# A seven-product matmul chunk with its products in another order

## The chip, the cores and the metric

The kernel runs on one core of one Trainium2 chip. TensorE (PE) multiplies, VectorE (DVE), ScalarE (ACT) and GpSimd (POOL) work on tiles beside it, and SyncE (SP) issues the transfers. The metric is the device time of one execution in microseconds: the median of three runs. Beside it stands one profiled execution with its trace.

## The reference

What is computed is one decoder layer in float32, and a last norm, over 1024 tokens of width 1024:

```python
def sqrelu_mlp(h, w1, w2):
    return jnp.square(jax.nn.relu(h @ w1)) @ w2

x = x + gla_mixer(rms_norm(x, norm_mix), w_in, w_gk_up, b_gk, g_onorm, w_out)
x = x + sqrelu_mlp(rms_norm(x, norm_ffn), w_ff1, w_ff2)
return rms_norm(x, final_norm)
```

The mixer is gated linear attention with four heads. It ends with a product of its gated output (1024 x 1024) and `w_out` (1024 x 1024). The MLP multiplies the normed rows by `w_ff1` (1024 x 4096), takes the square of the positive part, and multiplies by `w_ff2` (4096 x 1024). `rms_norm` divides each row by the root of its mean square and multiplies it by a gain.

## The kernel before, in words

The first third of the run is the attention with its projections. The change does not touch it. Everything after it is nine large products of 1024 x 1024 by 1024 x 1024, called **chunks** here: chunk 0 is the projection through `w_out`, whose result is added to the rows of x and kept as `x1`; then come four pairs, of which one chunk goes up (a quarter of `w_ff1`, result: a quarter of the hidden layer, `hd`) and one goes down (the fitting quarter of `w_ff2`, result: added to `x1`). The list `plan` (L852 to L855) holds for each chunk its left and right side and its sink, the function that takes each finished block of results away.

**One chunk is seven products and not eight.** Each matrix is cut into 2 x 2 blocks of 512 x 512, named "11", "12", "21", "22", and the chunk is computed by the Strassen-Winograd scheme. A product has as operands a block or a sum of blocks, and the results are kept in seven running sums. `form` (L600) says what each product needs: numbers 0, 4 or 3, 5 take blocks as they are, others take the sum "t" or the blocks after "t" has been worked into them. Only the products 0 and 5 take blocks as they were loaded or computed on both sides; each of the others needs a sum on one side at least.

**A product** is 48 matmuls of 128x512: four column blocks ("lanes") of 128 by two halves of the inner dimension by two by three. There are three because each float32 operand is split in two parts of lower width, `hi` (a copy on ACT, L86) and `lo` (the rest, a subtraction on DVE, L87), and hi x hi, hi x lo and lo x hi are summed. A lane's sum lies in one bank of PSUM. `BANK = "UVUVUWU"` says to which of three families of banks each of the seven products adds: U has four banks of the kind "gl"; V and W have three of the kind "mm" and one "gl" each. There are five "gl" and three "mm" banks. Products of one family add to the same banks one after another, and after products 0 to 6 a sink reads the sums as they stand.

**What sets the order of the work.** On PE it is the order in which the code is written (`tc.manual_schedule` for PE). The other engines' queues are set by a scheduler that follows the order of the code and lets blocks marked `high_priority` go ahead. The loop at L889 runs over the chunks and, in each, over the products. Before a product is issued, `operand` issues the next one's sums (L623: weights' sums on POOL, activations' sums on DVE) and splits (L86, L87). So the operands of a product are made while the product before it runs. A weight's sums for the product after that one are issued there too. SP issues all transfers in order; the weights of the next chunk are loaded while the products 5 and 6 of a chunk run.

**Buffers.** A weight block lies in a tile "w8" (three buffers) or "v8" (two); the sum "t" of the weights takes a "w8" buffer. Sums of activations lie in "raw" tiles, split operands in "big" tiles (eight), the hidden layer and the normed rows of the first up chunk in "og" tiles.

**The norm between.** After chunk 0 the rows of `x1` are normed (`normed`, L756: add, square on ACT, root, scale on DVE) and turned around by transposes on PE (`transposed`, L764: four transposes of 128x128 fill one "mm" bank, and ACT copies it out at L773). Rows 0 to 3 are complete when product 5 has been added, rows 4 to 7 with product 6. The up chunk needs the turned rows as its right operand.

**The end.** In the last chunk the sink is `final` (L822): it adds to `x1`, takes the squares of one half of a row when that half is complete, and finishes the row (root, scale, two transfers out) with the other half.

Of the kernel before, what the change touches and what calls it, by code (L numbers as in the profile page):

```python
# [14 lines left out]
ALU = mybir.AluOpType  # L15
# [33 lines left out]
def hybrid_trunk(ctx: ExitStack, tc: tile.TileContext, x, xT, w_head, w_r, w_gk, w_up,  # L49
# [85 lines left out]
    def run(general):  # L135
# [461 lines left out]
        BANK = "UVUVUWU"  # L597
        ADD, SUB = ALU.add, ALU.subtract
# [135 lines left out]
        wo.load("12")  # L734
# [87 lines left out]
        def final(n, lane, p_):  # L822
# [5 lines left out]
            if n in (3, 4):  # L828
                y = new(ROW[t])
                y, sq = row[t] = flat(y) if ROW[t] == "t2" else y, new("st")  # L830
                act.activation(y[:, 512:], xt[:, 512:], AF.Square, accum_out=sq[:, 0:1])
                pool.tensor_scalar(sq[:, 3:4], sq[:, 0:1], 1.0 / D, EPS, op0=ALU.mult, op1=ALU.add)
                pool.tensor_scalar(sq[:, 4:5], sq[:, 3:4], -0.5, None, op0=ALU.mult)
                pool.tensor_tensor(xt[:, 512:], xt[:, 512:], gfin[0][:, 512:], op=ALU.mult)
            elif n in (5, 6):
                y, sq = row[t]
                with tc.high_priority():
                    act.activation(y[:, :512], xt[:, :512], AF.Square, accum_out=sq[:, 1:2])
# [5 lines left out]
                    act.activation(y[:, 512:], xt[:, 512:], AF.Copy, scale=rs)  # L844
                    nc.sync.dma_start(out[t * P:(t + 1) * P, 512:], y[:, 512:])
                    dve.scalar_tensor_tensor(y[:, :512], xt[:, :512], rs, gfin[0][:, :512], op0=ALU.mult, op1=ALU.mult)
                    nc.sync.dma_start(out[t * P:(t + 1) * P, :512], y[:, :512])
# [35 lines left out]
        def transposes_after(hf):  # L883
            def between(lane):
                if lane in (1, 2):
                    transposed(hf, range(4 * lane - 4, 4 * lane))
            return between
# [101 lines left out]
```

## Time and profile before

| | |
|---|---|
| median of 3 runs | 1057.83 us (1057.79 to 1059.22) |
| profiled execution | 1058.82 us, span 1057.1 us |
| PE busy | 1034.1 us, 98%, 5122 matmuls and transposes |
| weight load (PEld) | 876.4 us, 83% |
| DVE, ACT, POOL busy | 717.8 us (68%), 535.0 us (51%), 245.1 us (23%) |
| transfers | 127.65 MB, mean 121 GB/s |

The span is what the profile covers; the profiled execution took 1.7 us more than that. Busy times are sums over the run, so they say which engine has work nearly always and not where an engine waits. For that the stretches of the run are read one by one. The attention ends at about 334 us; chunk 0 and its norms lie between 334 and 441 us; the up and down chunks fill the rest. In a row of the groups or of the timeline stand the start, the length, the engine, the line, the operation, the tiles `out<-in`, their shape and the count, and in brackets the idle time ahead of it with what ended it. A tile's name is cut to its kind there: `gl` and `mm` are banks of PSUM, `big` split operands, `w` and `v` weights, `raw`, `og`, `qk` activations.

### The profile page before, as it was taken

The numbers are of one execution on the slowest core, as the hardware profiler recorded it, in microseconds if no ns is written. First come the engines' busy times: TensorE is split into PE (matmuls) and PEld (weight loads), VectorE is DVE, ScalarE is ACT, GpSimd is POOL, SyncE is SP. The second block draws the span as 40 slices with busy tenths as digits, with TensorE's granted clock in tenths as the row PEclk, the third lists the DMA queues.
The fourth block names the chain that finished last, engine by engine and source line by source line (L and its number), as shares of the span: only waits on it lengthen the run. The fifth ranks groups of instructions, "written<-read, shape, count | busy, mean of one in ns | idle before, by whom it ended". The sixth has DMA issues, their size and how long they took to land.

```text
span 1057.1 us, 13350 instructions
## 1 busy us (share of the span) xinstructions
PE 1034.1 (98%) x5122; PEld 876.4 (83%) x5122; DVE 717.8 (68%) x960; ACT 535.0 (51%) x922; POOL 245.1 (23%) x151
## 2 busy tenths in 40 slices
PE   9999999999999898989999999999999999999996
PEld 8989899899888787778888888888888888888885
DVE  7564747566658986788997336986329976249975
ACT  2645747576656244856733245533346432447355
POOL 0000101000002604324223403404312406222351
PEclk9999999999999998999999999999999999999999
DMA  8510111112115140287222656123664043753004
GB/s 290 201 41 21 44 38 40 41 41 80 61 40 200 40 120 15 96 337 262 67 65 62 272 200 238 40 80 120 226 259 171 20 120 112 285 201 119 1 1 162
DMA packets 61977, 127.65 MB, mean 121 GB/s; under 512 B 3920, under 2 KB 36816, under 8 KB 54736
## 3 DMA queue, kind: packets, MB, share of 16 engines
q1 hardware_dynamic: 61760, 126.70, 33.9%
q8 instruction: 42, 0.69, 0.3%
q14 instruction: 31, 0.25, 0.1%
q10 hardware_dynamic: 144, 0.01, 0.0%
HBM read 107.82 MB, written 18.87 MB: 120 GB/s over the span
## 4 chain that ended last, share of the span: by engine, by line
PE 89%; DVE 6%; ACT 2%; issue 2%; DMA 1%; SPq 0%; ACTq 0%; DVEq 0%
PE gl L77 46%; PE mm L77 41%; DVE big L87 2%; DVE raw L623 2%; DMA w<-in_w_out 1%; PE gl L461 1%; DVE og L623 0%; ACT qk L759 0%; DMA raw<-in_w_head 0%; DVE t L726 0%; DVE qk L726 0%; PE gl L363 0%; PE mm L771 0%; DVE qk L761 0%; ACT og L773 0%
## 5 line engine op out<-in xcount | busy, mean ns | idle before, releaser
L77 PE MATMUL gl<-big,big 128*128 128x512 f32 x2052 | 480.6, 392 | 5.8 <-DVE big L87 5.8
L77 PEld LDWEIGHTS gl<-big,big 128*128 128x128 f32 x2052 | 388.1, 189 | 87.6 <-DVE big L87 6.6
L77 PE MATMUL mm<-big,big 128*128 128x512 f32 x972 | 229.7, 389 | 0.6 <-DVE big L87 0.5
L77 PEld LDWEIGHTS mm<-big,big 128*128 128x128 f32 x972 | 182.3, 188 | 39.1 <-DVE big L87 1.4
L87 DVE TENSOR_TENSOR big<-w,big 128x1024 fp32r<-128x1024 f32 x90 | 130.7, 1482 | 96.6 <-ACT big L86 96.6
L77 PE MATMUL mm<-big,w 128*128 128x512 f32 x744 | 180.5, 393 | 0.8 <-ACT w L86 0.8
L86 ACT ACTIVATE big<-w 128x1024 fp32r<-128x1024 f32 x90 | 91.1, 1052 | 142.0 <-PE gl L77 141.5
L77 PEld LDWEIGHTS mm<-big,w 128*128 128x128 f32 x744 | 136.4, 188 | 27.3 <-ACT w L86 1.0
L623 POOL TENSOR_TENSOR w<-w,w 128x1024 f32<-128x1024 f32 x36 | 107.6, 2998 | 136.6 <-DVE big L87 126.5
L623 POOL TENSOR_TENSOR w<-w,v 128x1024 f32<-128x1024 f32 x18 | 45.8, 2557 | 313.4 <-DVE big L87 140.1
L87 DVE TENSOR_TENSOR big<-v,big 128x1024 fp32r<-128x1024 f32 x36 | 52.0, 1469 | 50.4 <-ACT big L86 50.4
L87 DVE TENSOR_TENSOR big<-og,big 128x1024 fp32r<-128x1024 f32 (+1 forms) x52 | 57.5, 1115 | 32.3 <-ACT big L86 32.1
L77 PE MATMUL mm<-w,big 128*128 128x256 f32 x576 | 73.0, 284 | 0.0
L86 ACT ACTIVATE big<-og 128x1024 fp32r<-128x1024 f32 (+1 forms) x52 | 47.4, 953 | 49.6 <-PE gl L77 49.4
L77 PEld LDWEIGHTS mm<-w,big 128*128 128x128 f32 x576 | 70.9, 192 | 0.2
L86 ACT ACTIVATE big<-raw 128x1024 fp32r<-128x1024 f32 (+1 forms) x42 | 38.6, 933 | 60.6 <-DVE raw L623 40.5
L623 POOL TENSOR_TENSOR w<-v,w 128x1024 f32<-128x1024 f32 x18 | 57.0, 3185 | 43.2 <-DVE big L87 43.2
L87 DVE TENSOR_TENSOR big<-raw,big 128x1024 fp32r<-128x1024 f32 (+1 forms) x42 | 61.4, 1481 | 0.0
L86 ACT ACTIVATE big<-v 128x1024 fp32r<-128x1024 f32 x36 | 36.2, 1049 | 38.0 <-PE gl L77 38.0
L86 ACT ACTIVATE w<-raw 128x1024 fp32r<-128x1024 f32 (+2 forms) x26 | 25.7, 993 | 39.6 <-PE mm L77 27.5
L794 ACT ACTIVATE og<-og 128x1024 f32<-128x1024 f32 x24 | 25.4, 1058 | 39.6 <-DVE og L787 39.6
L87 DVE TENSOR_TENSOR w<-raw,w 128x1024 fp32r<-128x1024 f32 (+2 forms) x26 | 29.6, 1141 | 14.1 <-ACT w L86 13.8
(206 smaller groups left out, 1017.6 us busy)
## 6 DMA issues: line engine op xcount, KB each, us to landing
big<-xv SPq DMA_DIRECT2D x42, 1024.0 KB, 6.8
xv<-big SPq DMA_DIRECT2D x14, 1024.0 KB, 5.1
v<-in_w_ff SPq DMA_DIRECT2D x32, 256.0 KB, 4.4
w<-in_w_ff SPq DMA_DIRECT2D x32, 256.0 KB, 3.8
w<-in_w_ff SPq DMA_DIRECT2D x16, 512.0 KB, 5.5
v<-in_w_ff SPq DMA_DIRECT2D x16, 512.0 KB, 4.4
raw<-in_w_head SPq DMA_DIRECT2D x15, 512.0 KB, 4.0
og<-in_x SPq DMA_DIRECT2D x8, 512.0 KB, 7.6
```

The costliest lines, as they stand in the source:

```text
L77: pe.matmul(o, w, m, start=start, stop=stop, skip_group_check=partial)
L86: act.activation(hi, src, AF.Copy)
L87: dve.tensor_tensor(lo, src, f32(hi), op=ALU.subtract)
L461: pe.transpose(tp[:, j * P:(j + 1) * P], on[:, j * P:(j + 1) * P], ident)
L623: self.eng.tensor_tensor(*(self.ap(b, kp, self.span) for b in (o, x_, y_)), op=op)
L794: act.activation(d2, d2, AF.Relu)
```

## The change

The seven products of each chunk are issued in the order 0, 5, 1, 2, 3, 4, 6 and no longer by their numbers. Below, "place" means the position in that order and a product's number its number in `form`. Products 0 and 5, which take plain blocks, now stand first and second. With that:

- a lane's bank is taken when its first matmul is issued, and no longer all four at the start of a product;
- the loads of the next chunk's weights go out as "11" and "12" at the sixth place and "21" and "22" at the seventh; in chunk 0 "21" is loaded second, where "12" was, and "12" and "22" follow after the rows of x;
- weights' sums for place k + 1 are issued together with the operands of place k, in every chunk (the first up chunk had an order of its own);
- rows 0 to 3 of `x1` are complete after product 3 (the fifth place) and their norm moves there; the norm of rows 4 to 7 stays with product 6;
- the transposes of rows 0 to 3 move from two groups of sixteen, inside the seventh product of chunk 0, to four groups of eight: two in the sixth and two in the seventh. Those of rows 4 to 7 move from two groups of sixteen in the first product of the up chunk to four groups of eight, two in its first and two in its second product;
- in `final` the halves of a row change roles where the other half is complete first.

```diff
         BANK = "UVUVUWU"
+        ORDER = (0, 5, 1, 2, 3, 4, 6)
...
-            if n in (0, 1, 5):
-                for lane in range(4):
-                    bank[b, lane] = new("gl" if b == "U" or lane == 3 else "mm")
+            def take(lane):
+                bank[b, lane] = new("gl" if b == "U" or lane == 3 else "mm")
 
             def products(lane, kh):
+                if n in (0, 1, 5) and kh == 0:
+                    take(lane)
...
         wo.load("11")
-        wo.load("12")
+        wo.load("21")
         ops = [(so.split(0), wo.split(0))]
         for t in (0, 4, 1, 5, 2, 6, 3, 7):
             load_x1(t)
-        wo.sums(1)
         for f in r3[4:]:
             f()
+        wo.load("12")
         wo.load("22")
-        wo.load("21")
...
-        def operand(i, n):
+        def operand(i, at):
 
             out = []
             for s in plan[i][:2]:
                 early = s is weight_of(i)
-                if n and not early:
-                    s.sums(n)
-                out.append(s.split(n))
-                if n < 6 and early:
-                    s.sums(n + 1)
+                if not early:
+                    s.sums(ORDER[at])
+                out.append(s.split(ORDER[at]))
+                if at < 6 and early:
+                    s.sums(ORDER[at + 1])
             return out
 
-        def norm_after(e):
+        def norm_after(last, e):
             def then(n, lane, p_):
                 onto_x1(n, lane, p_)
-                normed(4 * e + lane)
+                if n == last:
+                    normed(4 * e + lane)
             return then
...
+        between = {(0, 5, 2): (0, (0, 1)), (0, 5, 3): (0, (2, 3)), (0, 6, 0): (0, (4, 5)), (0, 6, 1): (0, (6, 7)),
+                   (1, 0, 2): (1, (0, 1)), (1, 0, 3): (1, (2, 3)), (1, 1, 0): (1, (4, 5)), (1, 1, 1): (1, (6, 7))}
 
         for i, (lhs, rhs, sink) in enumerate(plan):
-            for n in range(7):
+            for at, n in enumerate(ORDER):
                 cur = ops.pop(0)
-                if n == 5:
-                    load(i + 1, ("11", "12", "22") if i % 2 else ("11", "21", "22"))
-                if n == 6:
-                    load(i + 1, ("21",) if i % 2 else ("12",))
...
+                here = {lane: between[i, at, lane] for lane in range(4) if (i, at, lane) in between}
+                if at == 5:
+                    load(i + 1, ("11", "12"))
+                if at == 6:
+                    load(i + 1, ("21", "22"))
...
+                following = (i, at + 1) if at < 6 else (i + 1, 0)
+                if following[0] < len(plan):
+                    ops.append(operand(*following))
+                if i == 0 and at in (4, 6):
+                    sink = norm_after(n, at // 6)
+                elif i == 0:
+                    sink = onto_x1
+                step(n, *cur, sink, bool(here) or i == len(plan) - 1 and at == 6,
+                     lambda lane: lane in here and transposed(*here[lane]))
```

The first place where the order differs is POOL's queue at the start of chunk 0, its first weight sums (the numbers behind a tile's kind tell the buffers' uses apart). Before:

```order
L623 TENSOR_TENSOR w8566_3545<-w8553_3510,v8552_3507 128x1024 x2
L623 TENSOR_TENSOR w8566_3545<-w8571_3612,w8566_3545 128x1024
L623 TENSOR_TENSOR w8553_3510<-w8571_3612,w8553_3510 128x1024
L623 TENSOR_TENSOR w8566_3545<-w8571_3612,w8566_3545 128x1024
L623 TENSOR_TENSOR w8553_3510<-w8571_3612,w8553_3510 128x1024
L623 TENSOR_TENSOR w8566_3545<-v8572_3615,w8566_3545 128x1024 x2
```

And now:

```order
L624 TENSOR_TENSOR w8578_3651<-w8570_3609,v8552_3507 128x1024 x2
L624 TENSOR_TENSOR w8570_3609<-w8571_3612,w8570_3609 128x1024 x2
L624 TENSOR_TENSOR w8578_3651<-w8571_3612,w8578_3651 128x1024 x2
L624 TENSOR_TENSOR w8578_3651<-v8553_3510,w8578_3651 128x1024 x2
```

The sums are the same eight. The sum "t" is now `w8578`, made after the blocks `w8570` and `w8571` and not before them, so it has another buffer: the one of the weights of the last attention projection (`w8549`), where before it was that of the projection ahead of it (`w8545`).

The second place is PE around the end of chunk 0 and the transposes of rows 4 to 7 in the up chunk. Before, with the first and last of a group of sixteen:

```order
L77 MATMUL gl661_4314<-big656_4295,big629_4142 128x512 x6
L77 MATMUL gl661_4314<-big657_4298,big630_4145 128x512 x6
L771 MATMUL mm668_4347<-ident_71,c4632_4164 128x128
...
L771 MATMUL mm671_4365<-ident_71,qk653_4285 128x128
L77 MATMUL gl662_4315<-big656_4295,big629_4142 128x512 x6
L77 MATMUL gl662_4315<-big657_4298,big630_4145 128x512 x6
L771 MATMUL mm674_4386<-ident_71,c4632_4164 128x128
...
L771 MATMUL mm677_4404<-ident_71,qk653_4285 128x128
```

And now, from the third group on, in the second product of the up chunk, with the first and last of a group of eight:

```order
L77 MATMUL mm680_4423<-big660_4309,big657_4300 128x512 x6
L77 MATMUL mm680_4423<-big661_4312,big658_4303 128x512 x6
L772 MATMUL mm683_4439<-ident_71,c4639_4195 128x128
...
L772 MATMUL mm684_4445<-ident_71,qk654_4290 128x128
L77 MATMUL mm685_4451<-big660_4309,big657_4300 128x512 x6
L77 MATMUL mm685_4451<-big661_4312,big658_4303 128x512 x6
L772 MATMUL mm686_4467<-ident_71,c4639_4195 128x128
...
L772 MATMUL mm687_4473<-ident_71,qk654_4290 128x128
L77 MATMUL mm688_4479<-big660_4309,big657_4300 128x512 x6
```

The groups are half as long, and here the product around them has its own sums in "mm" banks (`mm680`, `mm685`, `mm688`), as the transposes have, where before it was a product with sums in "gl" banks.

The third place is ACT's queue there, the copies of those transposes (L774). Before, they stood in two groups of four (L773), and a split between:

```order
L773 ACTIVATE og667_4346<-mm670_4359,vec_63 128x512
L773 ACTIVATE og667_4346<-mm671_4365,vec_63 128x512
L86 ACTIVATE big680_4427<-raw678_4423 128x2x512
L785 ACTIVATE og665_4330<-gl662_4315 128x512
L773 ACTIVATE og672_4384<-mm674_4386,vec_63 128x512
```

And now:

```order
L774 ACTIVATE og668_4362<-mm673_4395,vec_63 128x512
L86 ACTIVATE big678_4415<-raw676_4411 128x2x512
L86 ACTIVATE big679_4418<-raw677_4412 128x2x512
L774 ACTIVATE og681_4437<-mm683_4439,vec_63 128x512
L774 ACTIVATE og681_4437<-mm684_4445,vec_63 128x512
```

Two splits of sums (`raw676`, `raw677`) now stand between the second and the third pair of copies.

More of the change, by code (lines that the diff above doesn't have):

```diff
@@ L827, in final @@
             onto_x1(n, lane, p_)
-            if n in (3, 4):
+            if n in (4, 5):
                 y = new(ROW[t])
                 y, sq = row[t] = flat(y) if ROW[t] == "t2" else y, new("st")
-                act.activation(y[:, 512:], xt[:, 512:], AF.Square, accum_out=sq[:, 0:1])
+                cs = half(dh)
+                act.activation(y[:, cs], xt[:, cs], AF.Square, accum_out=sq[:, 0:1])
                 pool.tensor_scalar(sq[:, 3:4], sq[:, 0:1], 1.0 / D, EPS, op0=ALU.mult, op1=ALU.add)
                 pool.tensor_scalar(sq[:, 4:5], sq[:, 3:4], -0.5, None, op0=ALU.mult)
-                pool.tensor_tensor(xt[:, 512:], xt[:, 512:], gfin[0][:, 512:], op=ALU.mult)
-            elif n in (5, 6):
+                pool.tensor_tensor(xt[:, cs], xt[:, cs], gfin[0][:, cs], op=ALU.mult)
+            elif n in (3, 6):
                 y, sq = row[t]
+                cs, was = half(dh), half(1 - dh)
                 with tc.high_priority():
-                    act.activation(y[:, :512], xt[:, :512], AF.Square, accum_out=sq[:, 1:2])
+                    act.activation(y[:, cs], xt[:, cs], AF.Square, accum_out=sq[:, 1:2])
                     act.activation(sq[:, 6:7], sq[:, 1:2], AF.Ln, scale=1.0 / D, bias=sq[:, 3:4])
@@ L843, in final @@
                     dve.scalar_tensor_tensor(rs, sq[:, 7:8], 1.5, sq[:, 6:7], op0=ALU.add, op1=ALU.mult)
[L844 to L847, printed above, removed]
+                    act.activation(y[:, was], xt[:, was], AF.Copy, scale=rs)
+                    nc.sync.dma_start(out[t * P:(t + 1) * P, was], y[:, was])
+                    dve.scalar_tensor_tensor(y[:, cs], xt[:, cs], rs, gfin[0][:, cs], op0=ALU.mult, op1=ALU.mult)
+                    nc.sync.dma_start(out[t * P:(t + 1) * P, cs], y[:, cs])
         hd = [{} for _ in range(NC)]
@@ L889, in run @@
         for i, (lhs, rhs, sink) in enumerate(plan):
[L890 removed]
+            for at, n in enumerate(ORDER):
                 cur = ops.pop(0)
[L892 to L896 removed]
+                here = {lane: between[i, at, lane] for lane in range(4) if (i, at, lane) in between}
[3 more added lines that the diff above has]
+                    load(i + 1, ("21", "22"))
+                if i == NC * 2 - 2 and at == 0:
@@ L897, in run @@
                     gfin.append(new("c4"))
                     nc.sync.dma_start(gfin[0], g_fin)
-                if i == 0 and n == 6:
-                    w = plan[1][0]
-                    first_ = w.split(0)
-                    w.sums(1)
-                    step(n, *cur, norm_after(1), True, transposes_after(0))
-                    ops.append((first_, plan[1][1].split(0)))
-                elif i == 1 and n == 0:
-                    w = plan[1][0]
-                    second = w.split(1)
-                    w.sums(2)
-                    step(n, *cur, sink, True, transposes_after(1))
-                    plan[1][1].sums(1)
-                    ops.append((second, plan[1][1].split(1)))
-                else:
-                    if n < 6:
-                        ops.append(operand(i, n + 1))
-                    elif i + 1 < len(plan):
-                        ops.append(operand(i + 1, 0))
-                    step(n, *cur, norm_after(0) if i == 0 and n == 5 else sink, i == len(plan) - 1 and n == 6)
+                following = (i, at + 1) if at < 6 else (i + 1, 0)
```

6 lines of the change are left out of this document (removed).

## The prediction

> **What bounds the kernel now.** I read four views: the busy table of the page, the stretches of the middle of the run, the timeline inside them, and the chain of waits for the length of one matmul.
>
> The page first:
>
> ```profile
> PE 1034.1 (98%) x5122; PEld 876.4 (83%) x5122; DVE 717.8 (68%) x960; ACT 535.0 (51%) x922; POOL 245.1 (23%) x151
> PEclk9999999999999998999999999999999999999999
> ```
>
> and the length of one product's work, from the chain:
>
> ```profile
> 578.12 23.12 PE gl L77 x102
> ```
>
> TensorE is busy for 98% of the span, so time can be won only where it stands. The chain shows the pace without a gap: 102 matmuls in 23.12 us, 0.2267 us each, and a product of 48 takes 10.88 us. The line of the granted clock shows one dip, in slice 16, at 396 to 423 us.
>
> The stretches (us; then the busy time of PE, weight load, DVE, ACT and POOL with instruction counts; granted clock; DMA share and GB/s):
>
> ```profile
> 470.52:1034.90 564.38, 564.38 (x2491) 467.48 (x2490) 384.25 (x352) 260.16 (x305) 179.95 (x80) 1.00 0.39 139
> ```
>
> That row is the steady part; these are the stretches ahead of it:
>
> ```profile
> 344.80:356.40 11.60, 11.52 (x51) 9.01 (x49) 11.60 (x10) 2.52 (x4) 9.13 (x4) 1.00 0.23 56
> 356.40:359.30 2.90, 0.27 (x2) 0.02 (x1) 2.90 (x5) 0.64 (x1) 0.00 (x0) 1.00 0.03 6
> 359.30:364.50 5.20, 5.20 (x16) 4.13 (x17) 5.20 (x5) 1.26 (x2) 5.20 (x2) 0.67 0.01 2
> 364.50:371.70 7.20, 7.20 (x34) 5.93 (x32) 7.20 (x10) 4.53 (x7) 1.52 (x1) 1.00 0.00 0
> ...
> 410.60:417.80 7.20, 3.90 (x17) 3.12 (x17) 4.45 (x16) 2.00 (x6) 0.00 (x0) 0.74 0.00 0
> 417.80:423.90 6.10, 6.10 (x31) 5.07 (x29) 2.86 (x3) 4.02 (x7) 0.00 (x0) 0.75 0.34 137
> ...
> 432.10:440.80 8.70, 7.18 (x45) 5.69 (x45) 8.70 (x13) 6.25 (x10) 5.05 (x1) 1.00 0.00 0
> ...
> 454.70:458.10 3.40, 0.23 (x1) 0.00 (x0) 3.40 (x3) 3.17 (x5) 1.16 (x1) 1.00 0.42 178
> 458.10:463.50 5.40, 5.37 (x17) 4.26 (x18) 5.40 (x5) 0.81 (x1) 0.00 (x0) 0.68 0.90 358
> ```
>
> From 470.5 to 1034.9 us PE never stands: there is nothing to win in the eight chunks' steady part, only something to lose. Everything lies before it. In 356.4 to 359.3 PE does nothing and DVE is full, and the clock is 0.67 for the next 5.2 us. The same pair, a stall and a slow clock, stands at 454.7 and 458.1. In 410.6 to 417.8 PE does 3.9 us of work in 7.2 and in 432.1 to 440.8 it does 7.2 in 8.7: the two norms and their transposes.
>
> How much all this is: the two ends of the stretch, the start of the fourth product, and two pairs of transposes in a row.
>
> ```profile
> 333.91 11.17 PE L77 MATMUL gl<-big,big 128*128 128x512 f32 x48
> ...
> 372.56 1.66 PE L77 MATMUL mm<-big,big 128*128 128x512 f32 x6 [0.48 <-DVE big L87]
> ...
> 422.94 0.38 PE L771 MATMUL mm<-ident,c 128*128 128x128 f32 x2
> 423.16 0.38 PE L771 MATMUL mm<-ident,qk 128*128 128x128 f32 x2
> ...
> 470.52 4.24 PE L77 MATMUL mm<-big,big 128*128 128x512 f32 x18
> ```
>
> From the first matmul of the projection through w_out (333.91) to the fourth product of the first up chunk (470.52) are 136.6 us. The work in it is 10 products, 480 matmuls x 0.2267 = 108.8, and 64 transposes, four every 0.44 us or 0.11 each, 7.0: 115.8. **The loss is 20.8 us**, and it is the most that the change can win there. By place: third product 2.9 of stall (the row of 356.4) and 1.7 of clock (5.2 x 0.33); fourth 0.9 (it starts at 371.7 and goes on at 372.56); third product of the up chunk 3.2 (3.40 less the 0.23 of one matmul) and 1.7 (5.4 x 0.32). The second norm: 432.1 to 440.8 are 8.7 us for 32 transposes (3.5) and 13 matmuls (2.9), so 2.3. The first norm: from the end of the matmuls of 403.75 (a row further on), 410.6, to 423.87 are 13.3 us with 32 transposes and 12 matmuls (6.2), so 7.1, of it 5.4 the first row's (7.2 less 16 transposes). Small gaps make the rest, 1.0.
>
> **The change, term by term.** The number of products, sums, splits and transposes stays; only their places move. So I ask for each of the five places when its operands are ready and when PE wants them.
>
> What DVE and POOL take there:
>
> ```profile
> 328.63 5.00 POOL L623 TENSOR_TENSOR w<-w,v 128x1024 f32<-128x1024 f32 x2 [39.36 <-PE mm L77]
> 331.98 2.21 DVE L520 TENSOR_TENSOR t<-t 128x512 f32<-128x512 f32 x1 [2.18 <-ACT t L519]
> 336.51 0.68 DVE L516 TENSOR_TENSOR t<-mm,c 128x512 f32<-128x512 f32 x1
> 343.12 10.81 POOL L623 TENSOR_TENSOR w<-w,w 128x1024 f32<-128x1024 f32 x4 [9.49 <-DMA w<-in_w_out]
> 343.65 2.41 DVE L623 TENSOR_TENSOR raw<-og,qk 128x512 f32<-128x512 f32 x1
> 345.99 2.88 DVE L623 TENSOR_TENSOR og<-og 128x512 f32<-128x512 f32 x1
> 349.39 2.28 DVE L87 TENSOR_TENSOR big<-raw,big 128x512 fp32r<-128x512 f32 x1
> 352.20 2.28 DVE L623 TENSOR_TENSOR raw<-raw,og 128x512 f32<-128x512 f32 x1
> 358.01 2.35 DVE L87 TENSOR_TENSOR big<-w,big 128x1024 fp32r<-128x1024 f32 x2
> ```
>
> and the same stretch as a window:
>
> ```profile
> 331.98:359.20 27.22, 24.59 (x108) 19.65 (x106) 27.22 (x30) 10.14 (x15) 12.46 (x5) 1.00 0.59 213
> ```
>
> A DVE instruction of 128x512 takes a turn of 0.60 us (printed 0.68, they overlap), a split of 128x1024 takes 1.2 (two in 2.35). While POOL adds weight blocks (four in 10.81 us) DVE's instructions with both operands in SBUF take 2.41, 2.88, 2.28 and 2.28 us: about 1.75 us lost for each POOL add. As a check, count DVE's queue of before by these prices, from 331.98 to the first weights of the third product. The last row has 30 instructions, the last of them begun; 25 are short, 3 long and one tiny (0.1): 18.7 us. Four POOL adds cost 7.0, and the first instruction itself lost 1.5 (2.21 against 0.68). That gives 359.2, where the trace has PE's start at 359.28. The same prices carry the count of after.
>
> (a) *Second place, the product of the blocks "12" and "21".* It needs no sums and its splits stand early in DVE's queue: no stall, as before.
>
> (b) *Third and fourth place, the products that now need the sums.* POOL's first two adds (328.63, 5.00 us) ran while DVE had room. After the change their output buffer is the one that PE reads until 333.9, so they run in 333.9 to 338.9, in DVE's full stretch, and cost it 2 x 1.75. To the first weights of the third place DVE has 21 short, 3 long and the tiny one, 16.3 us, and four POOL adds, 7.0: 331.98 + 23.3 = 355.3, where PE wants them at 333.9 + 2 x 10.88 = 355.7. No stall (bounds: 0, and the 4.6 of before with its clock). To those of the fourth place come 14 short and 2 long, 10.8, and two POOL adds, 3.5: 369.6, where PE wants 366.5, so 3.1. A stall of 2.9 us was followed by a slow clock worth 1.7 (5.2 x 0.33); whether this one falls so is open, so 1.0 for it. Together 4.1 (bounds 0 without contention, and 6.7 with a whole POOL add lost each time and the full clock).
>
> The Trainium skill ("SBUF — State Buffer", who interferes with whom) says a VectorE instruction with two SBUF inputs and a GpSimd one that reads SBUF lock each other out, and one with a PSUM operand does not: it speaks against this change, which moves POOL adds into DVE's full stretch. The trace agrees: 2.41 us at 343.65 with both operands in SBUF, 0.68 at 336.51 with one in PSUM. By the rule taken to its end each of the six POOL adds costs its whole 2.7 us, 5.7 more in all, and the time would be 1053.1; by the rows it is the sum below. The same skill ("TensorE: Matmul & The Clock Gate", part 1) has the clock fall only after an idle window of some 3.4 us; here it fell after 2.9. By the page the sum would be 1 us smaller.
>
> (c) *First norm.* The rows that price it:
>
> ```profile
> 403.75 6.96 PE L77 MATMUL gl<-big,big 128*128 128x512 f32 x30
> 414.34 0.75 DVE L761 TENSOR_SCALAR qk<-L,rstd 128x1024 f32<-128x1024 f32 x1
> 423.87 8.45 PE L77 MATMUL gl<-big,big 128*128 128x512 f32 x36
> 433.13 1.41 DVE L761 TENSOR_SCALAR qk<-t,rstd 128x1024 f32<-128x1024 f32 x2
> ```
>
> The last column block of the product before the norm ended at 403.75 + 6 x 0.2267 = 405.1, its last normalised tile at 415.1: 10.0 us of add, square, root and scale, with PE waiting from 410.6. After the change that product is the fifth in order, and three column blocks of the next one (36 matmuls, 8.2 us) stand before the first transpose: 1.8 us of stall is left, and 0.6 for the clock. Bounds 0 and the old 7.1.
>
> (d) *Second norm.* It took 423.87 + 12 x 0.2267 = 426.6 to 434.5, 7.9 us. Now 8.2 us of products stand in between as well: 0 (bounds 0 and 2).
>
> (e) *Last transposes.* A split and a copy on ACT:
>
> ```profile
> 337.22 1.04 ACT L86 ACTIVATE big<-w 128x1024 fp32r<-128x1024 f32 x1
> ...
> 418.22 0.69 ACT L773 ACTIVATE og<-mm,vec 128x512 f32<-128x512 f32 x1 [0.17 <-PE mm L771]
> ```
>
> The transposes of the second norm now stand between the column blocks of a product that keeps its own sums in the same three "mm" banks. Its second block must wait until ACT has emptied a bank, and in ACT's queue two splits stand ahead, the second of which waits for a DVE sum. By the rows: copy 0.7, sum 1.2 (DVE, as its split of that size), split 1.05, copy 0.7, and hand-overs 0.3 make 3.9; PE has 2.7 + 0.9 = 3.6 in between. So 0.3 where POOL is quiet and 2.7 where DVE's sum meets a POOL add (2.4 more). POOL's next adds become free just then: I take 2.0, and 0.9 for the clock and the third block.
>
> (f) Small gaps: 1.0. The stall of 3.2 and its 1.7 at 454.7 goes: the sums of the up chunk now have one product more ahead of them, 10.9 us.
>
> Sum of what is left: 4.1 + 2.4 + 0 + 2.9 + 1.0 = 10.4. Gain: 20.8 - 10.4 = 10.4 us. Against the profiled execution (1058.82 us; span 1057.1 and 1.7 around it) that is 1048.4; its time stood 1.0 above the median of the runs, 1057.83, so **1047.4** for a median.
>
> The end stays: the last product is still the one that closes rows four to seven, and from its last add to the last output the same instructions follow.
>
> ```profile
> 1047.72 0.68 DVE L726 TENSOR_TENSOR t<-gl,t 128x512 f32<-128x512 f32 x1
> 1051.56 0.40 SPq L847 DMA_DIRECT2D out_y<-og  x1
> ```
>
> **Rivals.**
>
> *It turns out slower: banks at the new neighbours.* Products that follow each other on the same banks now come at three borders of a chunk (second to third, sixth to seventh, seventh to first) and not at one. A matmul of a column block may start only when the block's old sums are read.
>
> ```profile
> 588.45 2.45 DVE L87 TENSOR_TENSOR big<-w,big 128x1024 fp32r<-128x1024 f32 x1
> 590.82 1.28 DVE L726 TENSOR_TENSOR t<-gl,t 128x512 f32<-128x512 f32 x2
> ```
>
> This is the border that exists already. The chain's row holds 6 matmuls of the sixth product, 48 of the seventh and 48 of the next chunk's first, so the seventh ends at 578.12 + 1.36 + 10.88 = 590.4; the third block's add ended at 591.5, and PE wanted its bank at 590.4 + 2.7 = 593.1. So 1.6 us were to spare, with a POOL add in the way (2.45 at 588.45). At two more borders in each of the seven chunks behind the stretch, 14, the gain of 10.4 is gone once each costs 0.74 us, which takes an add that is 2.3 us later than here; at 1.5 each it is 21 us and the time 1068. Against it: in after's DVE queue the adds at the new borders stand behind splits whose buffers come free in mid product, as here.
>
> *The stall only moves.* The queue of DVE is as long as before, and if (b) keeps the 5.5 of before and (c) its 7.1, and (e) costs 5.0, then with (f) 18.6 us are left: a gain of 2.2, 1055.6. For it: DVE is at 100% in each row from 344.8 to 371.7, so what is late stays late. Against: one product more, 10.9 us, stands ahead of each sum.
>
> *All of it goes.* With (b) and (c) at 0 and (e) at 0.3, only 1.3 us are left and the time is 1038.3. For it: each of the three misses by less than 3 us.
>
> *The move does nothing* is not open: the order of products changes on PE itself, where it is written out.
>
> **How the numbers follow.** Forecast (gain 4 to 17 us) 0.69, of it 0.12 for the case that each of the six POOL adds of (b) costs DVE its whole 2.7 us instead of 1.75, 5.7 us more and 1053.1; all of it goes 0.06; the stall only moves 0.14; slower by the banks 0.11. About 0.2%, 2.1 us, is what a measurement here can tell from no change. Of the moving stall half lies within it, so faster 0.82, same 0.07, slower 0.11. The range 1040.5 to 1055.5 leaves out the slower cases and the full gain, and reaches to the moving stall.
>
> **What would show it.** Right: the row of 454.7 shows no stall; PE's first real stall comes at some 366 us and not 356; DVE stays at 100% to some 370; the rows behind the stretch hold PE at its full length; the stretch from the first w_out matmul to the fourth up product is about 126 us. Wrong: gaps of PE that repeat in each chunk, or a third place that still waits for DVE.

## The result

| | before | changed |
|---|---|---|
| median of 10 runs each | 1058.99 us (1057.79 to 1061.06) | 1062.18 us (1060.88 to 1063.5) |
| profiled execution, span | 1057.1 us | 1060.8 us |

The ratio is 1.0028 with a 95% interval of 1.0019 to 1.0038: the change makes the kernel slower, by 3 us. The forecast was 1047.4 and faster.

The busy table and the clock of the changed kernel's page:

```profile
PE 1034.4 (98%) x5122; PEld 875.8 (83%) x5122; DVE 718.7 (68%) x960; ACT 537.8 (51%) x922; POOL 243.9 (23%) x151
PEclk9999999999999899999999999999999999999998
```

PE is busy for the same time to 0.3 us. The dip of the clock has moved from slice 16 to slice 14, at 345 to 371 us. PE's timeline there, and the waits that stand behind it (the product's first row, its length and count, and in brackets the idle time and what ended it):

```profile
335.85 11.17 PE L77 MATMUL gl<-big,big 128*128 128x512 f32 x48
346.86 4.24 PE L77 MATMUL mm<-big,big 128*128 128x512 f32 x18
...
363.17 2.90 PE L77 MATMUL mm<-big,big 128*128 128x512 f32 x6 [5.27 <-DVE qk L728]
368.61 4.68 PE L77 MATMUL mm<-big,big 128*128 128x512 f32 x12 [2.54 <-DVE qk L728]
...
378.58 12.40 PE L77 MATMUL gl<-big,big 128*128 128x512 f32 x54
...
436.92 0.33 PE L772 MATMUL mm<-ident,qk 128*128 128x128 f32 x1 [1.22 <-DVE qk L762]
...
447.67 4.41 PE L77 MATMUL mm<-big,big 128*128 128x512 f32 x12 [2.76 <-ACT og L774]
...
453.29 3.02 PE L77 MATMUL mm<-big,big 128*128 128x512 f32 x12 [0.34 <-ACT og L774]
...
468.39 11.95 PE L77 MATMUL gl<-big,big 128*128 128x512 f32 x52
```

The stretch that the prediction counted goes from 335.85 to the fourth product of the first up chunk, which begins six matmuls into the last row, at 468.39 + 6 x 0.2267 = 469.75: **133.9 us, 2.7 less than before and not 10.4**. Its largest loss is at the third place of chunk 0. The product should start at 335.85 + 2 x 10.88 = 357.6; the fourth starts at 378.58 + 1.36 = 379.9. That is 11.4 us more than one product's work: two waits, 5.27 and 2.54, and some 3.4 us that the half clock costs. Both waits end with `DVE qk L728`, and that is neither a sum nor a split: it is the add that takes the second product's sums out of their banks.

Behind the stretch, from its end to the end of the span, the changed kernel takes 1060.8 - 469.75 = 591.05 us and the kernel before 1057.1 - 470.52 = 586.6: **4.4 us lost** in a part that had no wait before. In each down chunk there is now one, at the border of the second and third place, and the last chunk has a second:

```profile
535.58 4.37 PE L77 MATMUL mm<-big,big 128*128 128x512 f32 x18 [0.39 <-DVE qk L728]
...
995.08 4.37 PE L77 MATMUL mm<-big,big 128*128 128x512 f32 x18 [0.39 <-DVE qk L728]
999.83 1.65 PE L77 MATMUL gl<-big,big 128*128 128x512 f32 x6 [0.38 <-DVE L L728]
```

The first three cost 0.68 us each (from 533.67, where six matmuls begin, to 535.58 are 1.91 us and not 1.36; inside the row of 18 are 0.13 more), the last chunk 1.3; some small gaps cost 0.5, and the end, from PE's last matmul to the last output, 0.5.

What is left of the 3.7 us between the two spans lies at the front: the projection starts at 335.85 and not at 333.91. PE's instructions are the same up to there. The first matmuls ran at half clock for longer in this execution, as the same four matmuls of the kernel before and of the changed one show:

```profile
6.14 0.65 PE L77 MATMUL gl<-w,big 128*128 128x256 f32 x4
```
and in the changed kernel
```profile
6.75 1.06 PE L77 MATMUL gl<-w,big 128*128 128x256 f32 x4
```

So it is + 1.9 at the front, - 2.7 in the stretch and + 4.4 behind it. The whole of the 1.9 arises in the first 13 us, in instructions that are the same in both kernels, and in other traces of kernels with the new order in chunk 0 it lies between 0 and 1.9; so it is put down to chance here.

### The profile page after: what moved, and what is told of

Its sections match the earlier page's. It is cut to its first block, busy times and chain, and to the rows that moved or that the text cites. A ratio compares the mean times of both kernels' runs of the same rounds, so it can differ in the third digit from the quotient of the medians.

```text
span 1060.8 us, 13321 instructions
## 1 busy us (share of the span) xinstructions
PE 1034.4 (98%) x5122; PEld 875.8 (83%) x5122; DVE 718.7 (68%) x960; ACT 537.8 (51%) x922; POOL 243.9 (23%) x151
## 4 chain that ended last, share of the span: by engine, by line
PE 82%; DVE 12%; ACT 3%; issue 1%; DMA 0%; SPq 0%; ACTq 0%; DVEq 0%
PE gl L77 44%; PE mm L77 37%; DVE big L87 6%; DVE raw L624 3%; DVE qk L728 1%; ACT big L86 1%; PE gl L461 1%; DVE L L728 0%; DVE qk L522 0%; DVE t L520 0%; DMA raw<-in_w_head 0%; ACT t L518 0%; PE gl L363 0%; ACT t L519 0%; ACT t L517 0%
## 5 line engine op out<-in xcount | busy, mean ns | idle before, releaser
L77 PE MATMUL mm<-big,big 128*128 128x512 f32 x972 | 234.8, 395 | 12.5 <-DVE qk L728 9.4
L77 PEld LDWEIGHTS mm<-big,big 128*128 128x128 f32 x972 | 184.8, 191 | 54.1 <-issue 8.8
L87 DVE TENSOR_TENSOR big<-w,big 128x1024 fp32r<-128x1024 f32 x90 | 125.3, 1424 | 99.9 <-ACT big L86 99.9
L624 POOL TENSOR_TENSOR w<-w,w 128x1024 f32<-128x1024 f32 x36 | 112.6, 3146 | 227.8 <-DVE big L87 223.6
L87 DVE TENSOR_TENSOR big<-og,big 128x1024 fp32r<-128x1024 f32 (+1 forms) x52 | 64.3, 1244 | 51.3 <-ACT big L86 51.3
L87 DVE TENSOR_TENSOR big<-raw,big 128x1024 fp32r<-128x1024 f32 (+1 forms) x42 | 72.4, 1729 | 2.6 <-ACT big L86 2.6
L87 DVE TENSOR_TENSOR big<-v,big 128x1024 fp32r<-128x1024 f32 x36 | 48.2, 1354 | 36.4 <-ACT big L86 36.4
L624 POOL TENSOR_TENSOR w<-v,w 128x1024 f32<-128x1024 f32 x18 | 52.1, 2902 | 58.6 <-DVE big L87 58.6
```

Of the source, the lines that this page charges most:

```text
L77: pe.matmul(o, w, m, start=start, stop=stop, skip_group_check=partial)
L87: dve.tensor_tensor(lo, src, f32(hi), op=ALU.subtract)
L624: self.eng.tensor_tensor(*(self.ap(b, kp, self.span) for b in (o, x_, y_)), op=op)
```

## The experiments

The first theory (A) after the result: the third product stands on the same three "mm" banks as the second one, and its first matmuls wait for the adds that empty them; the adds are late because in DVE's queue they stand behind the sums and splits for the fourth place. DVE's timeline in the changed kernel:

```profile
357.07 2.35 DVE L87 TENSOR_TENSOR big<-w,big 128x1024 fp32r<-128x1024 f32 x2
359.34 1.88 DVE L624 TENSOR_TENSOR raw<-raw,og 128x512 f32<-128x512 f32 x3
361.14 0.68 DVE L624 TENSOR_TENSOR og<-og 128x512 f32<-128x512 f32 x1
361.74 0.68 DVE L87 TENSOR_TENSOR big<-raw,big 128x512 fp32r<-128x512 f32 x1
362.35 0.68 DVE L728 TENSOR_TENSOR qk<-mm,qk 128x512 f32<-128x512 f32 x1
362.95 5.00 DVE L87 TENSOR_TENSOR big<-raw,big 128x512 fp32r<-128x512 f32 x2
367.87 0.68 DVE L728 TENSOR_TENSOR qk<-mm,qk 128x512 f32<-128x512 f32 x1
```

The third product's own weights are split at 359.4 (the first row's end), 1.8 us late. But the first add comes at 362.35, 8.7 us after its sum was complete (the second product's first column block ends at 346.86 + 30 x 0.2267 = 353.7), and the second only at 367.87, behind two splits that take 5.00 us.

All kernels below are written with a table that gives each chunk its own order; with the changed kernel's order in all nine chunks it is that kernel. In the diffs `N` stands for the new order and `O` for the old one. The traces side by side, in us; a kernel whose name begins with "and" has the edits of the kernel above it as well; "stretch" is from the first matmul through `w_out` to the fourth product of the first up chunk, "behind" from there to the end of the span:

| kernel | first w_out matmul | stretch | behind | median of runs | ratio to before, 95% |
|---|---|---|---|---|---|
| before | 333.91 | 136.6 | 586.6 | 1058.99 | |
| changed | 335.85 | 133.9 | 591.0 | 1062.18 | 1.0028 (1.0019 to 1.0038) |
| chunk 0 old | 333.95 | 130.3 | 591.4 | 1057.26 | 0.9984 (0.9975 to 0.9994) |
| chunks 0, 1 new, rest old | 334.70 | 134.8 | 586.6 | 1057.86 | 0.9988 (0.9978 to 0.9998) |
| adds first | 334.26 | 126.4 | 591.0 | 1054.65 | 0.9958 (0.9944 to 0.9972) |
| sums early | 333.87 | 130.4 | 591.0 | 1057.23 | 0.9994 (0.9980 to 1.0008) |
| adds first, rest old | 335.23 | 126.3 | 587.2 | 1051.05 | 0.9934 (0.9911 to 0.9957) |
| and copies first | 335.76 | 124.8 | 587.2 | 1048.62 | 0.9900 (0.9878 to 0.9921) |
| and sums early | 335.56 | 121.9 | 586.7 | 1045.81 | 0.9873 (0.9855 to 0.9892) |
| down chunks old | 335.33 | 135.1 | 586.6 | 1056.88 | 0.9982 (0.9970 to 0.9993) |
| before, again | 334.45 | 136.3 | 586.6 | 1059.0 | one run |
| changed, again | 335.53 | 133.6 | 591.0 | 1061.82 | one run |

The medians are of 10 runs each, but of 5 with the adds first, of 4, 4 and 5 in the three rows that build on it. The ratio is to the kernel before as it ran beside them; its median was 1058.72 us beside the four kernels from "chunk 0 old" to "sums early" and 1058.94 beside the next four.

**Chunk 0 in the old order.**

```diff
-ORDERS = (N, N, N, N, N, N, N, N, N)
+ORDERS = (O, N, N, N, N, N, N, N, N)
-between = {(0, 5, 2): (0, (0, 1)), (0, 5, 3): (0, (2, 3)), (0, 6, 0): (0, (4, 5)), (0, 6, 1): (0, (6, 7)), ...}
+between = {(0, 6, 1): (0, (0, 1, 2, 3)), (0, 6, 2): (0, (4, 5, 6, 7)), ...}
```

The loads, the first sums and the splits around chunk 0 stand in their old places as well.

> Chunk 0 in the old order with the old norm and transposes of rows 0 to 3; all other chunks in the new one. Theory A (in chunk 0 the third product waits for the second one's sums to leave the three mm banks, 11.4 us with the slow clock behind it, and the down chunks wait 0.7 us each at the same border, while the first norm costs nothing any more): chunk 0 gets back 4.6 + 0.9 for its third and fourth product and 7.1 for the first norm and loses the 11.4: the stretch from the first matmul through w_out to the fourth product of the first up chunk is about 135 us (133.9 in the changed kernel), the down chunks keep their 0.7 each: 1 us slower than the changed kernel. Rival B (the new order in chunk 0 is the whole loss): 5 us faster than the changed kernel.

By the medians it was 4.9 us faster than the changed kernel, where theory A had it 1 us slower; rival B's number came out. The waits in the stretch, and ahead of them the wait of 2.63 in the kernel before:

```profile
359.28 12.57 PE L77 MATMUL gl<-big,big 128*128 128x512 f32 x47 [2.63 <-DVE big L87]
```
```profile
359.68 10.96 PE L77 MATMUL gl<-big,big 128*128 128x512 f32 x47 [2.63 <-DVE big L87]
372.97 4.16 PE L77 MATMUL mm<-big,big 128*128 128x512 f32 x17 [2.11 <-DVE big L87]
...
443.55 3.03 PE L77 MATMUL mm<-big,big 128*128 128x512 f32 x12 [1.01 <-ACT og L776]
```

The wait of 2.63 at the third place is the one of before to the hundredth, but here 47 matmuls behind it take 10.96 us, full speed; before, they took 12.57, the first of them at half clock. Counted from the starts of the products, the seven places of chunk 0 lose 12.4 us here and 11.5 in the changed kernel, so for chunk 0 itself theory A was near, with 1.6 us of luck in the clock. What it left out lies behind: the second norm costs nothing here and 1.4 us there, and the product with the last transposes loses 2.1 us and not 5.2, since the transposes wait 1.01, not 2.76, and at full clock. With that the new order in chunk 0 is a net loss. It is not the whole loss, as "behind" shows, which stays at 591. And one chunk stands out on the other side: with the new order in the first up chunk alone of the two, the stretch is 6.3 us shorter than before. The old wait of 3.2 us at 454.7 and its slow clock are gone in it; some 1.6 us of the 6.3 are the clock behind the wait of 2.63.

**The seven chunks behind in the old order, and the down chunks alone.**

```diff
-ORDERS = (N, N, N, N, N, N, N, N, N)
+ORDERS = (N, N, O, O, O, O, O, O, O)
```

> Chunks 0 and 1 as in the changed kernel, the seven chunks behind them in the old order. Theory A: the stretch stays at 133.9 us, the waits of 0.4 to 0.7 us in each down chunk are gone (4.0 us in all) and the end is as before (0.4): 4.4 us faster than the changed kernel, 1 to 2.7 us faster than the kernel before. Rival C (the small waits of the down chunks are paid anyway, by the last output): no faster than 1 us than the changed kernel.

```diff
+ORDERS = (N, N, O, N, O, N, O, N, O)
```

> The changed kernel with the old order in the four down chunks alone. Theory A (the 4.0 us behind the stretch are lost at the border of the second and third place of the down chunks, nowhere else): no wait of PE behind the stretch, 4.3 us faster than the changed kernel, as with the old order in all seven chunks. Rival I (up chunks lose as well): half of it.

Both came out as theory A has it: 4.3 and 5.3 us faster than the changed kernel, 586.6 us behind the stretch in both. (The stretch itself was about 1 us longer than in the changed kernel, 134.8 and 135.1, with the same waits and more half clock behind them.) With the old order in the down chunks alone PE has no wait there; this is that kernel's stretch as a window (PE's busy time is the window's whole length):

```profile
470.60:1035.00 564.40, 564.40 (x2491) 467.50 (x2490) 377.84 (x352) 258.88 (x306) 172.18 (x80) 1.00 0.39 143
```

So the up chunks lose nothing by the new order, and rivals C and I fall. Why the down chunks do, the changed kernel's trace shows at the first of them:

```profile
527.11 6.65 POOL L624 TENSOR_TENSOR w<-w,w 128x1024 f32<-128x1024 f32 x2 [36.75 <-DVE big L87]
528.08 3.42 DVE L624 TENSOR_TENSOR raw<-raw,og 128x1024 f32<-128x1024 f32 x1
...
531.42 3.42 DVE L87 TENSOR_TENSOR big<-raw,big 128x1024 fp32r<-128x1024 f32 x1
...
534.76 1.27 DVE L728 TENSOR_TENSOR qk<-mm,qk 128x512 f32<-128x512 f32 x2
535.96 1.21 DVE L87 TENSOR_TENSOR big<-raw,big 128x1024 fp32r<-128x1024 f32 x1
...
537.69 1.21 DVE L624 TENSOR_TENSOR raw<-og,raw 128x1024 f32<-128x1024 f32 x1
```

There DVE makes the sums of the hidden layer. Two of its instructions, which take 1.21 us each where POOL is quiet (535.96 and 537.69), take 3.42 while POOL adds weights, and the adds stand behind them. That the order makes the wait is shown by the two runs; that POOL's part in it is needed is read from this trace alone, since no run moved POOL's adds in a down chunk.

**The adds ahead of the sums, in chunk 0 alone.** The sums of activations for the fourth place may not go ahead of the second product's last add in DVE's queue; nothing else changes. (In the code, `last_add` holds the add that was issued last.)

```diff
                     for o, x_, op, y_ in self.form[n][1]:
-                        self.eng.tensor_tensor(...)
+                        made_ = self.eng.tensor_tensor(...)
+                        if behind[0] is not None and self.eng is dve:
+                            order_after(tc, made_, behind[0], wait=False)
...
+                behind[0] = last_add[0] if (i, at) == (0, 2) else None
```

> The changed kernel, but in chunk 0 the sums of activations for the product at the fourth place stand behind the second product's adds in DVE's queue. Theory A: the third product starts when its weights are split, some 1.7 us late and not 5.3, the second wait of 2.5 is gone, and the fourth place waits up to 3 us: the stretch is about 128 us, 6 us less than in the changed kernel, and the time 1056. Rival D (the adds are late since POOL's adds block DVE, whatever the order): the stretch stays at 133 to 134 us.

The stretch fell by 7.5 us to 126.4, the median by 7.5 to 1054.65. First DVE, then PE in this kernel:

```profile
353.83 2.35 DVE L87 TENSOR_TENSOR big<-w,big 128x1024 fp32r<-128x1024 f32 x2
356.09 1.88 DVE L732 TENSOR_TENSOR qk<-mm,qk 128x512 f32<-128x512 f32 x3
357.89 0.68 DVE L732 TENSOR_TENSOR L<-gl,L 128x512 f32<-128x512 f32 x1
358.48 2.84 DVE L625 TENSOR_TENSOR raw<-raw,og 128x512 f32<-128x512 f32 x1
```
```profile
356.92 4.37 PE L77 MATMUL mm<-big,big 128*128 128x512 f32 x18 [0.61 <-DVE qk L732]
...
370.33 2.50 PE L77 MATMUL gl<-big,big 128*128 128x512 f32 x5 [2.02 <-DVE big L87]
```

The four adds now stand right behind the weights' splits. The wait at the third place is 0.61 where it was 7.8, and one of 2.02 appears at the fourth. This undoes the order of DVE's queue and nothing else, and it takes away all but 0.6 us of the wait: theory A is shown for chunk 0, and rival D falls as the only cause. Not all of the 7.5 us is the edit's. Counted from the starts of the products, the third and fourth place together lose 6.5 us less, the two norms 0.4 more, and the product with the last transposes 1.4 less. Its wait is as long as in the changed kernel (2.76 us), but the 12 matmuls behind it took 3.02 us and not 4.41: in this execution the clock did not fall there, and that part is luck.

**POOL's first two weight sums early.** Block "12" is loaded ahead of "22" and the sum is issued where it was before.

```diff
             load_x1(t)
+        wo.load("12")
+        wo.sums(1)
         for f in r3[4:]:
             f()
-        wo.load("12")
         wo.load("22")
...
-                if at < 6 and early:
+                if at < 6 and early and (i, at) != (0, 1):
```

> The changed kernel, but POOL's first two weight sums run where they ran before (the blocks 12 and the sum are placed ahead of block 22), while DVE has room. Theory A: DVE is 3.5 us earlier, the third product's first wait falls from 5.3 to about 2 and the second stays near 2.5, since the adds still stand behind splits for the fourth place: the stretch is about 130 us. Rival D (POOL is the cause): both waits go, 122 to 125 us. Rival E (adds wait only for buffers): 133 to 134 us.

The stretch was 130.4, as theory A gave it, but not by its steps. There was one wait and it was longer, 6.77 us:

```profile
353.54 6.04 POOL L625 TENSOR_TENSOR w<-w,w 128x1024 f32<-128x1024 f32 x2 [5.37 <-DVE big L87]
...
354.52 6.21 DVE L625 TENSOR_TENSOR raw<-raw,og 128x512 f32<-128x512 f32 x3
...
361.87 0.68 DVE L729 TENSOR_TENSOR qk<-mm,qk 128x512 f32<-128x512 f32 x1
362.69 3.75 PE L77 MATMUL mm<-big,big 128*128 128x512 f32 x8 [6.77 <-DVE qk L729]
```

DVE was earlier at the sums for the fourth place, but it met POOL's next two adds there, and three instructions took 6.21 us in place of 1.88. The add came at 361.87, which is 28.0 us after the first matmul through `w_out`, where it was 26.5 in the changed kernel. That the second wait went, and with it a part of the slow clock, won 2.1 of the 3.5 us; the other 1.4 are again the clock behind the last transposes, which did not fall in this execution. So the number of theory A came out by luck as well. POOL's contention adds to the delay. With the adds where the changed kernel has them in the queue, moving POOL's sums does not take the delay away.

**Everything that won, together.** First the adds ahead and the old order from the first down chunk on:

```diff
+ORDERS = (N, N, O, O, O, O, O, O, O)      # with the adds ahead in chunk 0
```

> Two edits together: the second product's adds ahead of the sums for the fourth place in chunk 0, and the old order in the seven chunks from the first down chunk on. Theory A (the two losses are independent): the stretch from the first matmul through w_out to the fourth product of the first up chunk stays at 126 to 127 us, no wait behind it; 4.3 us less than with the first edit alone, about 1050.3. Rival F (what is won in front is given back by later waits): no more than 1 us less.

1051.05 and a stretch of 126.3: the two losses are independent, and rival F falls. ("Behind" is 0.6 us longer here than in the kernel before, and so it is with the next edit: one product of the third up chunk starts 0.5 us late in both, of it 0.3 as a wait. Why, no run shows.) Then the transposes in the up chunk. Between its column blocks ACT's copies, which empty the "mm" banks of the transposes, stood behind two splits that wait for DVE's sums; now the splits stand behind the copies, and they are issued behind the step, with the sums that they split.

```diff
-LATE = ()
+LATE = ((1, 1),)
...
-        act.activation(hi, src, AF.Copy)
+        made_ = act.activation(hi, src, AF.Copy)
+        if last_copy[1]:
+            order_after(tc, made_, last_copy[0], wait=False)
```

> The same two edits, and in the first up chunk ACT's splits of the sums for the third place stand behind the copies of the last transposes. Theory A (those copies wait behind splits that wait for sums): the wait of 2.76 us in the second product of the up chunk and the 0.34 behind it fall to under 1 us together, the stretch is about 124 us, 2.3 us less than without. Rival G (the copies wait for the three mm banks' transposes themselves): the wait stays near 2.7. Rival H (the splits are late then): the wait goes to the third place of the up chunk, the time stays.

The stretch was 124.8, 1.5 less, where 2.3 were expected. The wait fell from 2.76 and 0.34 to one of 1.69, not to under 1, with another releaser:

```profile
439.52 0.68 DVE L797 TENSOR_TENSOR og<-mm,og 128x512 f32<-128x512 f32 x1
...
440.26 3.02 PE L77 MATMUL mm<-big,big 128*128 128x512 f32 x12 [1.69 <-DVE og L797]
```

It is now the product's own sum in the third bank, which DVE has to add to the hidden layer, behind a sum that meets POOL (3.11 us for 128x1024). Of rivals G and H neither is right: it is the same shortage of banks with its next user. Last, with POOL's first sums early as well:

```diff
+        wo.load("12")
+        wo.sums(1)
```

> The three edits, and POOL's first two weight sums where they ran before. Theory A: with DVE 3.5 us earlier the wait of 2.0 us at the fourth place of chunk 0 and the slow clock behind it go: the stretch is 120 to 121 us and the time about 1044. Rival D (the fourth place waits for the sums of activations, which now stand behind the adds): the wait stays at 2 us, stretch 123 to 124, 1047.

Stretch 121.9, **1045.81 us, 0.9873 of the kernel before (0.9855 to 0.9892)**: 13 us faster than before and 16 faster than the changed kernel. PE starts the third place without a wait, and the one of 2.0 us at the fourth is gone:

```profile
356.08 1.52 PE L77 MATMUL gl<-big,big 128*128 128x512 f32 x6
357.44 1.30 PE L77 MATMUL mm<-big,big 128*128 128x512 f32 x5
...
380.31 0.96 PE L77 MATMUL mm<-big,big 128*128 128x512 f32 x3 [0.59 <-DVE big L91]
```

The same edit, of which 2.1 us could be counted when the adds were late, saves 2.9 of the stretch here, now by the step that was expected of it. Theory A's 120 to 121 is missed by 1 us; what is left over the 115.8 of pure work is the 1.7 above, 1.0 and 0.8 at the two norms, 0.6 at the fifth place, and small gaps.

**The two kernels once more, unchanged.**

> The kernel before once more, unchanged, for a second trace of it. Theory K (whether the granted clock falls behind a stall of 2 to 3 us depends on where the stall falls in time, not on its length): PE's waits stand at the same places with the same lengths to 0.1 us, but the half clock follows other ones of them, and the stretch from the first matmul through w_out to the fourth product of the first up chunk differs from 136.6 us by up to 3 us. Rival L (the length decides): half clock behind the same waits, stretch 136.6 within 0.3.

> The changed kernel once more, unchanged. Theory K: waits of 5.3, 2.5, 1.2 and 2.8 us as before, the stretch between 132 and 136 us by the clock behind the last of them; the start of the first matmul through w_out between 333.8 and 336 us, by how long the first matmuls run at half clock. Rival L: stretch 133.9 within 0.3.

The waits were the same to 0.15 us in both, and the stretches 0.3 us shorter than in the first traces (136.3 and 133.6). So rival L's number holds, and half clock follows the same waits. In the kernel before, though, it does not hold as long behind them: in the second trace the seventh product of chunk 0, with the first norm, lost 1.3 us less than in the first, and the third product of the up chunk 1.1 us more. That the two nearly cancel is luck, and the last section shows waits behind which the half clock is a matter of chance. The front took 334.45 and 335.53: over the twelve traces it lies between 333.87 and 335.85 us with the same instructions.

## Why the prediction was wrong, point by point

**The step that failed is (b)**, "To the first weights of the third place ... No stall". The count of DVE's queue behind it was short by 2.2 us: it gave 355.3 against a need at 355.7, which is 357.2 against 357.6 with this execution's start, and the weights were ready at 359.4. That alone would have been a wait of 1.8 us. But the third product needs two things: its operands and its banks. The prediction asked only for the operands in chunk 0. The banks' wait was written down as a rival, with the right mechanism, and priced for "each of the seven chunks behind the stretch" from a place where DVE had time to spare. In chunk 0, where the same text shows DVE busy for all 27.22 of 27.22 us, it was not priced. (b) was to cost 4.1 us, all of it at the fourth place; it cost 11.4 at the third and nothing at the fourth. The prediction's own signs of being wrong both came: gaps of PE that repeat, in each down chunk, and a third place that waits for DVE.

**The argument against that rival was wrong too.** "Adds at the new borders stand behind splits whose buffers come free in mid product, as here": in chunk 0 the splits ahead of the adds were for the fourth place, and they met POOL. In the down chunks two DVE instructions of 1.21 us became 3.42. The rival's own price was 0.74 to 1.5 us at 14 borders; measured were five waits in four down chunks, 3.3 us in all, and no wait from the sixth to the seventh and from the seventh to the first product. So that rival was right in kind and about a third of its smallest price.

**(a)** held: no wait at the second place. **(c)** the first norm was to keep 2.4 and kept 0 in the changed kernel; with the earlier waits gone, in the last experiment, it kept 1.0. **(d)** was to cost 0 and cost a wait of 1.2, 1.4 with small gaps. **(e)** was right in its mechanism, the copies behind ACT's splits, and short in size: 2.9 forecast; measured were 2.76 and 0.34 of waiting and some 2.1 of slow clock and small gaps, 5.2. **(f)** the wait of 3.2 us in the up chunk went as forecast, with its slow clock.

The sum of what was left in the stretch was forecast as 10.4 and was 18.1. The rival *the stall only moves* had 18.6, near to it for another reason. With the adds put ahead the stretch is 126.4, where the forecast's own sum, 136.6 - 10.4, gives 126.2. That is closer than its parts deserve: (b) then costs 4.9 against 4.1, (c) about 0.8 against 2.4, (d) 1.1 against 0 and (e) 3.8 against 2.9, and (e) had the luck of a full clock, without which it is 5.2. Still, the wait for the banks, which the sum did not hold, is most of the 7.7 us that separate the forecast from the result in the stretch. The rest of the way from the forecast to the result is the 4.4 us behind the stretch and the 1.9 at the front.

One reading of the lines was off as well. The "2.9 of stall" is the length of a window in which PE is busy for 0.27 us; the wait itself is 2.63, as the row of 359.28 says, so the slow clock followed a wait of 2.63 and not of 2.9.

**What stays open.** The first pair of traces gives the changed kernel 1.7 us more than before once the front is left out, and so does the second pair. The medians differ by 3.2, with an interval from 2.0 to 4.0. The front and the clock behind each wait vary by about 2 us from one execution to the next, and a few traces do not settle where the last 1.5 us lie. Two things on record bear on it. Of the three traces with the old order in chunk 0 none starts the projection later than 334.45, while the nine others reach 335.85, so it is not shown that the front is pure chance. And the clock granted to each run has a median of 0.9885 over the ten runs of the changed kernel and 0.991 over 41 runs of the kernel before.

## What to carry to other kernels

When products are put in another order, ask two questions of each new pair of neighbours, and ask them in every stage: when are the operands ready, and when has the last reader left the banks. The reader stands in a queue, so count what stands ahead of it there; in a stage where that engine is full, the wait is as long as the queue and not as long as the instruction. And a queue that a scheduler fills can be put right with one order constraint: here four adds ahead of eight sums gave 7.5 us by the medians. When the gain of an edit is read from one pair of traces, sum it by place first: a part of it can be a clock that fell in one trace and not in the other.

## What the runs showed of the hardware

A wait of 2.0 us on PE is sometimes followed by half clock for 3.4 us, and sometimes not. The same wait at the same place, in the kernel with the adds ahead, and in the one with the old order behind it, whose first 470 us hold the same work; in each the two rows are the first piece of the product in a stretch and the stretch as a window (its granted clock is the third number from the end):

```profile
370.33 2.50 PE L77 MATMUL gl<-big,big 128*128 128x512 f32 x5 [2.02 <-DVE big L87]
370.33:373.80 3.47, 3.47 (x8) 2.77 (x9) 3.47 (x4) 0.00 (x0) 2.37 (x1) 0.52 0.00 0
```
```profile
371.18 1.66 PE L77 MATMUL gl<-big,big 128*128 128x512 f32 x6 [2.03 <-DVE big L87]
371.18:374.60 3.42, 3.42 (x15) 2.85 (x16) 3.42 (x3) 0.00 (x0) 2.40 (x1) 1.00 0.00 0
```

Eight matmuls against fifteen in 3.4 us: 1.6 us lost or not, for the same wait. The waits of 2.63 and 2.76 us show both outcomes as well. And the half clock can hold for longer. The wait ahead of the last transposes' product, in the kernel with the adds ahead and in the one with the old order in the down chunks:

```profile
439.96 3.02 PE L77 MATMUL mm<-big,big 128*128 128x512 f32 x12 [2.76 <-ACT og L779]
```
```profile
446.88 5.49 PE L77 MATMUL mm<-big,big 128*128 128x512 f32 x12 [2.71 <-ACT og L775]
```

In the second the granted clock is half from 446.2 to 453.0, 6.8 us or two times 3.4, and the product loses 2.8 us more. In the changed kernel it is half from 361.9 to 372.2, 10.2 us or three times 3.4, through both waits of the third product. The Trainium skill ("TensorE: Matmul & The Clock Gate", part 1) says that the activity is watched in windows of 3.4 us that run freely and do not start with the kernel, so that the number of slow matmuls at a kernel's start changes from run to run. The traces agree with the free-running window and its length. The condition that the Trainium skill gives there, an idle window of 3.4 us, is not needed in full: 2.0 us of waiting were enough when they fell right. The prediction read it as a threshold and wrote that by it the clock would not fall; a price for a wait of 2 to 3 us here is its length plus 0, some 1.5 or, once, 2.8 us. What PE loses so is not always lost for the run: of the two kernels at 370 us above, the one that kept its clock waited 0.6 us for DVE at the fifth place and 0.7 longer at the first norm, and the two stretches are 126.4 and 126.3.
